# A two-layer trunk on one core: later last quarter products and inner tiles in the MLP batches, plain tiles behind its heads, ada pieces moved

## The chip, the cores and the metric

The kernel runs on one core of a Trainium2 chip. A core has a matrix engine (TensorE, PE in the profile; PEld is its weight load), VectorE (DVE), ScalarE (ACT), GpSimd (POOL) and SyncE (SP), whose queue issues nearly all DMAs here. The metric is the device time of one execution in microseconds (us).

## The reference

Two residual layers on x of 512 positions by 1024 features, in fp32. Cut to what matters:

```python
for layer in range(DEPTH):                      # DEPTH = 2
    mod = c_act @ ada_w[layer] + ada_b[layer]
    shift1, scale1, gate1, shift2, scale2, gate2 = jnp.split(mod[:, None, :], 6, axis=-1)
    h = rms_norm(x, norm_mix[layer]) * (1.0 + scale1) + shift1
    if layer % 2 == 0:
        y = mixer_conv_hgrn(h, ...)             # gated convolution and HGRN2 recurrence
    else:
        y = mixer_stick_breaking(h, ...)        # causal attention without softmax
    x = x + gate1 * y
    h = rms_norm(x, norm_mlp[layer]) * (1.0 + scale2) + shift2
    x = x + gate2 * (jnp.square(jax.nn.relu(h @ mlp_w1[layer])) @ mlp_w2[layer])
```

The MLP of each layer goes from 1024 to 4096 and back. The change lies mostly in it.

## The kernel before

**Products.** Activations lie transposed: 128 features by 512 positions in a tile. Every fp32 product is three matmuls (`mm3`, L276 to L283): both operands are split into a high and a low part, and hi x hi (L281), hi x lo (L282) and lo x hi (L283) are summed in a PSUM bank. A weight tile of 128x1024 (512 KB, eight blocks of 128 columns) is loaded by SP into one of three raw slots (`raw_w`, L258); ACT copies it to the high part (L271), DVE subtracts for the low part (L272); `whi` and `wlo` have four slots each. The split weights start at the slot's first byte (`AT512`) or 64 bytes on (`AT256`, L265): those of products with 512 columns have the first, those with 256 columns the second.

**Ada pieces.** `mod` is made in pieces of 128 outputs: a 512 KB load into a raw slot on SP and one dot on DVE (L420, with a short read of its sum). `background(n)` puts the next n pieces in at its place in the order. In layer 0's mixer there are 4 pieces behind v_g, one behind each of the four lin heads, one behind each lin of the four conv tiles and one at the end of each, and 8 between the first three tiles of the output projection and the fourth. In layer 0's MLP there are two behind each w2 tile until none is left, that is in batches 0 to 2.

**The MLP.** The 32 hidden tiles are made in four batches of eight; after each batch its share of the second product is added to x. Hidden tiles 0 to 3 of a layer are the head (`mlp_head`, L1149, and L1627 for layer 1): by halves of 256 positions, with direct products, while `sums` (L1007) builds from h four tiles of sums t0 to t3 on DVE and ACT. All other hidden tiles come in pairs (`pair`, L1065): a two-by-two Strassen-Winograd scheme makes two hidden tiles with seven quarter products of 12 matmuls of 256 columns (84) in place of 96. Its weights are made on DVE (`pair_w`, sums L1058 to L1062, splits L272). The seven go into three banks a, b and c in this order: hh, t0, t1, hh, hh, t2 and at last t3. ACT copies intermediate sums out, DVE adds them at L1104 and L1106 (both halves of the first tile) and L1109 (the second half of the second tile, from bank a). The seventh product, t3 with `wd`, adds to bank a again, so it waits for L1109. It is deferred: `pair` returns it, and the next pair runs it as `before()` behind its second product. After each half or tile ACT takes relu and square and copies the high part (`hidh`), DVE subtracts (`hidl`, L291).

**A batch's end.** In `mlp` (L1117) the deferred product of the last pair is run by `rest()`, and then the w2 tiles follow: eight in batches 0 to 2, five in batch 3 (the other three are made by halves in the code behind it). Each has eight inner tiles k = 0 to 7 (the batch's hidden tiles), three matmuls of 512 columns each, and then `x_add` (L506, DVE reads the bank), and `background(2)`.

**Order.** In layer 0 and in both MLPs the order on PE is that of the code. On DVE, ACT and SP a scheduler places the instructions, so that a change on PE shifts them. Banks are given by `acc`, which counts up through eight names.

Of the kernel before, what the change touches and what calls it, by code (L numbers as in the profile page):

```python
# [23 lines left out]
P = 128  # L24
T = 512
NT = 8
# [194 lines left out]
def trunk(tc, x_d, c_d, rep_d, small_d, const_d, ada_d, ws_d, win_d, wv_d, woab_d, w1_d, w2_d, wqk_d, wvc_d, woc_d, out_d):  # L221
# [53 lines left out]
    def load_w(src, of=None, at=AT512):  # L275
        return split_w(raw_w(src), of, at)  # L276

    def mm3(ps, w, wc, h, hs, start, stop, **kw):

        whi, wlo = w[0][:, wc], w[1][:, wc]  # L280
        pe.matmul(ps, whi, h[0][:, hs], start=start, stop=False, **kw)  # L281
        pe.matmul(ps, whi, h[1][:, hs], start=False, stop=False, **kw)  # L282
        pe.matmul(ps, wlo, h[0][:, hs], start=False, stop=stop, **kw)  # L283
# [68 lines left out]
    def acc():  # L352
        return mps.tile([P, T], F32, name="acc", tag="acc", bufs=4)
# [94 lines left out]
    def background(n):  # L448
        for _ in range(min(n, len(todo))):
            l, v, f = todo.pop(0)  # L450
            ada_piece(l, v, f)
            if f == 7:
                ada_done(l, v, 0, 8)
# [469 lines left out]
    background(4)  # L923
    for h in range(4):
        run(lin(h, do_hg, h))
        background(1)


    def conv(i):
        p3 = []  # L930
        for r in range(3):
            yield from lin(4 + 3 * i + r, p3.append)
            background(1)
            if r == 0:
                cv = mp.tile([P, T], F32, name="cv", tag="cv", bufs=2)
                act.copy(cv, p3[0])
            elif r == 1:
                u = mp.tile([P, T + 2], F32, name="u", tag="u")
                pool_e.memset(u[:, 0:2], 0.0)
                dve.tensor_tensor(u[:, 2:T + 2], p3[1], cv, op=ALU.mult)  # L940
                cw = [small[:, S_CONV + 4 * r + i:S_CONV + 4 * r + i + 1] for r in range(3)]
                dve.tensor_scalar(cv, u[:, 2:T + 2], cw[2], None, op0=ALU.mult)
                dve.scalar_tensor_tensor(cv, u[:, 1:T + 1], cw[1], cv, op0=ALU.mult, op1=ALU.add)
                dve.scalar_tensor_tensor(cv, u[:, 0:T], cw[0], cv, op0=ALU.mult, op1=ALU.add)
        dve.tensor_tensor(cv, p3[2], cv, op=ALU.mult)
        yy = mp.tile([P, 2, T], F32R, name="yy", tag=f"y{i}")
        yh, yl = yy[:, 0], yy[:, 1]
        split(cv, yh, yl)
        y[i] = (yh, yl)
        background(1)  # L950

    for i in range(4):
        run(conv(i))
# [18 lines left out]
    HALVED = (4, 5, 6, 7)  # L972
    PLACES = {5: (mp, "F2", "Q2"), 6: (mp, "Ft", "Kt")}
    run(proj((0, 1, 2), [load_w(woab_d[o]) for o in (0, 1, 2)], FULL))
    background(8)
    for o in range(3, HALVED[0]):
        run(proj((o,), [load_w(woab_d[o])], FULL))
    ws = {o: load_w(woab_d[o], PLACES.get(o), AT256) for o in HALVED}
# [11 lines left out]


    pp = pool("pp", PSUM)
    bank = [0]

    def acc(n=T):
        bank[0] += 1
# [71 lines left out]
    def pair(l, i, hp, th, hid, before):  # L1068
# [45 lines left out]
            relu2(1, H[0], a)  # L1114
        return last

    def mlp(l, last, hp, head, th):  # L1117

        nrm = Norm(1, 0, (7,)) if not last else None
        for b in range(4):  # L1120
            hid, rest = list(head) if b == 0 else [], lambda: None
            for i in range(len(hid) // 2, 4):
                rest = pair(l, 4 * b + i, hp, th, hid, rest)
            rest()
            for o in range(8 if b < 3 else 5):
                w, ps = load_w(w2_d[l, b // 2, o, b % 2]), acc()
                for k in range(8):
                    mm3(ps, w, ks(k), hid[k], FULL, k == 0, k == 7)
                x_add(o, ps, FULL, l, GATE2)
                if b == 3:  # L1130
                    if last:
                        sync.dma_start(out_d[o], x[o])
                    else:
                        nrm.add(o, FULL)
                background(2)
        if not last:
            log_exp_tables()
        ps, banks, ws = {}, {}, []
        for o in range(5, 8):
            for hf in range(2):  # L1140
                banks[bank[0] % 8] = o, hf
                ps[o, hf] = acc(256)

            ws.append(load_w(w2_d[l, 1, o, 1], None if o == 5 else (hp, f"t{o - 6}h", f"t{o - 6}l"), AT256))
        return nrm, ps, banks, hid, ws
# [480 lines left out]

    w = [weights(w1_d[1, j], None, AT256) for j in range(4)]  # L1627
    for hf, sl in enumerate(H):
        ps = [r.new() for r in (accs, accs, zts, zts)]
        for k, j in by_half(hf, 4):  # L1630
            order.append(mm3h(ps[j], half, w[j], ks(k), (hh[hf][k],), sl, k == 0, k == NT - 1, 256))
        for j in range(4):
            c_, (hi, lo) = cms.new(), hid[j]
            on_act(256, lambda c_=c_, p_=ps[j], sl=sl: act.activation(c_.t[:, sl], half(p_.t), AF.Relu), (ps[j],), (c_,), 0, psum=True)
            on_act(256, lambda c_=c_, sl=sl: act.activation(c_.t[:, sl], c_.t[:, sl], AF.Square), (c_,), (c_,), 0)
            on_act(256, lambda c_=c_, hi=hi, sl=sl: act.copy(hi.t[:, sl], c_.t[:, sl]), (c_,), (hi,), 0)
            on_dve(256, lambda c_=c_, hi=hi, lo=lo, sl=sl: dve.tensor_tensor(lo.t[:, sl], c_.t[:, sl], hi.t[:, sl].bitcast(F32),
                   op=ALU.subtract), (c_, hi), (lo,), 0)
# [87 lines left out]
```

## Time and profile before

| what | value |
|---|---|
| time, median of 3 runs | 1272.83 us (1272.48 to 1274.75) |
| the profiled execution's own time | 1269.31 us |
| its span | 1267.5 us |
| mean granted clock of TensorE | 0.984 |
| PE busy | 1224.1 us (97%) |
| DVE busy, ACT busy | 904.9 us (71%), 622.9 us (49%) |
| DMA | 163.50 MB, mean 129 GB/s |

In the span layer 0's lin and conv tiles lie from about 65 to 216 us, its projection to 263, the head of its MLP to 291.7; its batches end near 319, 406, 493 and 579. The attention of layer 1 starts at about 616, the head of its MLP at 913.8, and its batches end near 966, 1050, 1134 and 1218. A row of a timeline has the start, the duration, the engine, the line, the operation with its output and inputs, the shape, and in brackets the idle time of the engine before it with what ended that. Ends of matmuls are modelled, and they overlap; the step from one start to the next is what a matmul costs.

### The profile page before, as it was taken

Reading aid. Unit: us, or ns where it says so; the run is one execution under the profiler, and the core shown is the slowest. Engines: PE = TensorE matmul, PEld = TensorE weight load, DVE = VectorE, ACT = ScalarE, POOL = GpSimd, SP = SyncE. Lnnn points to the kernel's source line nnn. Section 1 sums busy time; section 2 is a strip of 40 time slices with the busy share of each in tenths; the row PEclk is TensorE's granted clock in tenths of the full one; section 3 lists DMA queues with packets and bytes.
Section 4 is the critical chain, followed back from the end, with each engine's and each line's share of the span. In section 5 each row is a group of like instructions: output and inputs, shape, how many; then the busy total and the mean of one; then the engine's idle time right before and its main releaser. Section 6 shows DMA issues by size and latency. Waiting matters only on the chain.

```text
span 1267.5 us, 19414 instructions
## 1 busy us (share of the span) xinstructions
PE 1224.1 (97%) x7721; PEld 1069.3 (84%) x7721; DVE 904.9 (71%) x1455; ACT 622.9 (49%) x1127; POOL 13.8 (1%) x24
## 2 busy tenths in 40 slices
PE   8999999998999999999999999999889999999998
PEld 6888878988798898898978778777888898998988
DVE  8996859679788688785567773669795575675651
ACT  4433232456247165275458754667465273372650
POOL 0000000000000000000200000000000000000000
PEclk9999999998999999999989999999999999999999
DMA  8664444613745736734132213322013233143141
GB/s 310 245 217 160 139 150 147 202 34 113 252 151 187 252 126 222 239 105 166 51 100 68 67 51 91 93 67 95 31 43 123 77 100 119 65 150 100 52 149 50
DMA packets 46618, 163.50 MB, mean 129 GB/s; under 512 B 5296, under 2 KB 6328, under 8 KB 46528
## 3 DMA queue, kind: packets, MB, share of 16 engines
q1 hardware_dynamic: 46384, 161.78, 38.5%
q8 instruction: 60, 0.98, 0.3%
q10 hardware_dynamic: 144, 0.49, 0.1%
q14 instruction: 30, 0.25, 0.1%
HBM read 155.96 MB, written 2.10 MB: 125 GB/s over the span
## 4 chain that ended last, share of the span: by engine, by line
PE 78%; DVE 12%; DMA 5%; ACT 3%; issue 2%; SPq 0%; DVEq 0%; ACTq 0%
PE b L281 17%; PE b L283 17%; PE b L282 17%; DMA wraw<-in_w 3%; PE acc L281 3%; PE acc L283 3%; PE acc L282 3%; DVE wlo L272 3%; PE acc L652 2%; PE b L1486 1%; PE b L1465 1%; PE b L1521 1%; ACT whi L271 1%; PE b L1385 1%; PE b L1522 1%
## 5 line engine op out<-in xcount | busy, mean ns | idle before, releaser
L271 ACT CAST whi<-wraw 128x1024 fp32r<-128x1024 f32 x123 | 127.8, 1048 | 238.7 <-DMA wraw<-in_w 103.8
L281 PE MATMUL b<-hidh,whi 128*128 128x512 f32 (+1 forms) x560 | 209.1, 373 | 0.0
L282 PE MATMUL b<-hidl,whi 128*128 128x512 f32 (+1 forms) x560 | 208.2, 372 | 0.0
L283 PE MATMUL b<-hidh,wlo 128*128 128x512 f32 (+1 forms) x560 | 207.8, 371 | 0.0
L281 PE MATMUL b<-hh,whi 128*128 128x256 f32 (+1 forms) x624 | 191.7, 307 | 6.2 <-DVE x L506 5.9
L272 DVE TENSOR_TENSOR wlo<-wraw,whi 128x1024 fp32r<-128x1024 f32 x123 | 150.4, 1223 | 61.4 <-ACT whi L271 59.5
L283 PE MATMUL b<-hh,wlo 128*128 128x256 f32 (+1 forms) x624 | 187.2, 300 | 1.9 <-DVE wlo L272 1.9
L282 PE MATMUL b<-hl,whi 128*128 128x256 f32 (+1 forms) x624 | 186.5, 299 | 0.0
L506 DVE SCALAR_TENSOR_TENSOR x<-b,modc,x 128x512 f32<-128x512 f32 (+1 forms) x102 | 68.8, 675 | 105.9 <-PE b L283 105.7
L281 PEld LDWEIGHTS b<-hh,whi 128*128 128x128 f32 x624 | 119.1, 191 | 18.3 <-issue 7.2
L283 PEld LDWEIGHTS b<-hh,wlo 128*128 128x128 f32 x624 | 118.9, 190 | 6.4 <-DVE wlo L272 2.3
L282 PEld LDWEIGHTS b<-hl,whi 128*128 128x128 f32 x624 | 119.8, 192 | 3.1
L282 PEld LDWEIGHTS b<-hidl,whi 128*128 128x128 f32 x560 | 106.1, 190 | 18.0
L281 PEld LDWEIGHTS b<-hidh,whi 128*128 128x128 f32 x560 | 105.8, 189 | 18.2
L283 PEld LDWEIGHTS b<-hidh,wlo 128*128 128x128 f32 x560 | 105.6, 189 | 18.4
L420 DVE CUSTOM_DVE_ANT_0 ascr<-wraw,cb 128x1024 bf16<-128x1024 f32 x80 | 97.8, 1222 | 22.1 <-DMA wraw<-in_ada 21.6
L272 DVE TENSOR_TENSOR wlo<-tt,whi 128x1024 fp32r<-128x1024 f32 x56 | 68.3, 1221 | 18.6 <-ACT whi L271 17.7
L271 ACT CAST whi<-tt 128x1024 fp32r<-128x1024 f32 x56 | 57.3, 1050 | 48.6 <-PE b L282 34.1
L1299 DVE TENSOR_TENSOR wlo<-raw,whi 128x1024 fp32r<-128x1024 f32 x34 | 41.5, 1222 | 21.8 <-ACT whi L1298 21.5
L281 PE MATMUL acc<-hh,whi 128*128 128x512 f32 x128 | 52.2, 408 | 0.0
L1449 DVE TENSOR_TENSOR_SCAN om<-om,pat 128x772 f32<-128x772 f32 (+2 forms) x24 | 46.5, 1936 | 5.8 <-ACT om L1445 5.8
L282 PE MATMUL acc<-hl,whi 128*128 128x512 f32 x128 | 49.9, 390 | 0.0
(376 smaller groups left out, 2709.6 us busy)
## 6 DMA issues: line engine op xcount, KB each, us to landing
wraw<-in_w SPq DMA_DIRECT2D x124, 512.0 KB, 3.4
wraw<-in_ada SPq DMA_DIRECT2D x80, 512.0 KB, 4.3
eraw<-in_ada SPq DMA_DIRECT2D x16, 512.0 KB, 3.9
wraw<-in_win SPq DMA_DIRECT2D x16, 512.0 KB, 3.3
raw<-in_wqk SPq DMA_DIRECT2D x16, 512.0 KB, 3.6
raw<-in_ws SPq DMA_DIRECT2D x8, 512.0 KB, 6.1
wraw<-in_woab SPq DMA_DIRECT2D x8, 512.0 KB, 3.9
raw<-in_wvc SPq DMA_DIRECT2D x8, 512.0 KB, 3.4
```

The costliest lines, as they stand in the source:

```text
L271: act.copy(hi, raw)
L272: dve.tensor_tensor(lo, raw, hi.bitcast(F32), op=ALU.subtract)
L281: pe.matmul(ps, whi, h[0][:, hs], start=start, stop=False, **kw)
L282: pe.matmul(ps, whi, h[1][:, hs], start=False, stop=False, **kw)
L283: pe.matmul(ps, wlo, h[0][:, hs], start=False, stop=stop, **kw)
L420: dve.tensor_tensor_reduce(out=scr, in0=raw, in1=cb, scale=1.0, scalar=0.0, op0=ALU.mult, op1=ALU.add, accum_out=modr[:, col:col + 1])
L506: dve.scalar_tensor_tensor(x[o][:, sl], ps, mcol(l, v, o), x[o][:, sl], op0=ALU.mult, op1=ALU.add)
L652: order.append(on("PE", 8 * 0.000417 * (sl.stop - sl.start), lambda k=k, wi=wi, hi_=hi_, sl=sl, w=w: [pe.matmul(sacc[j][:, sl], w[wi].t[:, ...
L1299: on_dve(1024, lambda: dve.tensor_tensor(lo.t, raw.t, hi.t.bitcast(F32), op=ALU.subtract), (raw, hi), (lo,), 1)
L1385: on_pe(0.13, lambda s=s, sq=sqs[p, s, s0]: pe.matmul(ms.t[64 + 32 * s:96 + 32 * s, sl], hs, sq.t[:, sl], start=True, stop=True), (sqs[p, ...
L1449: on_dve(2 * nw, lambda: dve.tensor_tensor_scan(s_(), s_(), pats[i][:, ::-1], 0.0, op0=ALU.mult, op1=ALU.max), (om,), (om,), 2)
L1465: pe.transpose(tp.t[:, o_:o_ + P], be.t[:, w0:w0 + P], ident)
```

## The change

Six edits:

1. Each of the four lin heads has two ada pieces behind it instead of one, and each conv tile two at its end instead of one; the eight ahead of the projection's fourth tile go. The number of pieces is the same.
2. The counter of bank names in the MLP of layer 0 starts at 4.
3. Hidden tiles 4 and 5 of each layer, right behind the head, are made directly (`whole_tile`): two times 24 matmuls of 512 columns, in place of a pair of 84 with 256.
4. The last deferred product of a batch comes behind inner tiles 0 to 6 of w2 tile 0; then come inner tiles 0 to 6 of w2 tile 1; then inner tile 7 of both, with their x_adds and ada pieces behind.
5. The weights of the last w2 tile of each batch start 64 bytes on.
6. In layer 1's head the fourth accumulator is taken from another ring of banks (`miscs` instead of `zts`).

```diff
     for h in range(4):
         run(lin(h, do_hg, h))
-        background(1)
+        background(2)
...
         y[i] = (yh, yl)
-        background(1)
+        background(2)
...
     run(proj((0, 1, 2), [load_w(woab_d[o]) for o in (0, 1, 2)], FULL))
-    background(8)
...
-    bank = [0]
+    bank = [4]
...
+    def whole_tile(l, j, hp, hid):
+
+        w, ps, c_ = load_w(w1_d[l, j]), acc(), hp.tile([P, T], F32, name="cm", tag="cm", bufs=3)
+        for k in range(NT):
+            mm3(ps, w, ks(k), hT[k], FULL, k == 0, k == NT - 1)
+        hid.append(hid_new(hp, j))
+        act.activation(c_, ps, AF.Relu)
+        act.activation(c_, c_, AF.Square)
+        split(c_, *hid[j])
+
     def mlp(l, last, hp, head, th):
...
             hid, rest = list(head) if b == 0 else [], lambda: None
+            if b == 0:
+                for j in (4, 5):
+                    whole_tile(l, j, hp, hid)
             for i in range(len(hid) // 2, 4):
                 rest = pair(l, 4 * b + i, hp, th, hid, rest)
-            rest()
-            for o in range(8 if b < 3 else 5):
-                w, ps = load_w(w2_d[l, b // 2, o, b % 2]), acc()
-                for k in range(8):
-                    mm3(ps, w, ks(k), hid[k], FULL, k == 0, k == 7)
+            n = 8 if b < 3 else 5
+            second = lambda o: (acc(), load_w(w2_d[l, b // 2, o, b % 2], None, AT256 if o == n - 1 else AT512))
+
+            def products(p, k0, k1):
+                for k in range(k0, k1):
+                    mm3(p[0], p[1], ks(k), hid[k], FULL, k == 0, k == 7)
+
+            def done(o, ps):
                 x_add(o, ps, FULL, l, GATE2)
...
-                background(2)
+                if b < 3:
+                    background(2)
+
+            p0 = second(0)
+            products(p0, 0, 7)
+            rest()
+            p1 = second(1)
+            products(p1, 0, 7)
+            for o, p in enumerate((p0, p1)):
+                products(p, 7, 8)
+                done(o, p[0])
+            for o in range(2, n):
+                p = second(o)
+                products(p, 0, 8)
+                done(o, p[0])
...
-        ps = [r.new() for r in (accs, accs, zts, zts)]
+        ps = [r.new() for r in (accs, accs, zts, miscs)]
```

PE at the end of batch 0 of layer 0, before (`b_2816` is bank a of the last pair):

```order
L282 MATMUL b_2816<-t2l,whi 128x256
L283 MATMUL b_2816<-t2h,wlo 128x256
L281 MATMUL b_2816<-t3h,wdh 128x256
L282 MATMUL b_2816<-t3l,wdh 128x256
L283 MATMUL b_2816<-t3h,wdl 128x256
```

Now (`b_2770` is that bank, `b_2868` the bank of w2 tile 0):

```order
L282 MATMUL b_2770<-t2l,whi 128x256
L283 MATMUL b_2770<-t2h,wlo 128x256
L281 MATMUL b_2868<-hidh,whi 128x512
L282 MATMUL b_2868<-hidl,whi 128x512
L283 MATMUL b_2868<-hidh,wlo 128x512
```

```order
L281 MATMUL b_2868<-hidh,whi 128x512
L282 MATMUL b_2868<-hidl,whi 128x512
L283 MATMUL b_2868<-hidh,wlo 128x512
L281 MATMUL b_2770<-t3h,wdh 128x256
L282 MATMUL b_2770<-t3l,wdh 128x256
L283 MATMUL b_2770<-t3h,wdl 128x256
```

The t3 product stood right behind that of t2 in the same bank; 21 matmuls of 512 columns now stand between them (the first three and the last three are shown).

DVE at the same place, before, from L1104 of the last pair on (`hidl` of 128x512 is the sixth inner tile, counted from 0; the rows of 128x256 are halves of the seventh):

```order
L1104 TENSOR_TENSOR cm<-b_2817,kept 128x256
L272 TENSOR_TENSOR wlo<-wraw,whi 128x1024
L1106 TENSOR_TENSOR cm<-b_2818,kept 128x256
L420 ISA ascr,modr<-wraw,cb 128x1024
L420 ISA modr 128x1
L1109 TENSOR_TENSOR cm<-b_2816,kept 128x256
L420 ISA ascr,modr<-wraw,cb 128x1024
L420 ISA modr 128x1
L291 TENSOR_TENSOR hidl<-cm,hidh 128x512
L291 TENSOR_TENSOR hidl<-cm,hidh 128x256
L272 TENSOR_TENSOR wlo<-wraw,whi 128x1024
L291 TENSOR_TENSOR hidl<-cm,hidh 128x256
```

Now:

```order
L272 TENSOR_TENSOR wlo<-wraw,whi 128x1024
L1104 TENSOR_TENSOR cm<-b_2771,kept 128x256
L420 ISA ascr,modr<-wraw,cb 128x1024
L420 ISA modr 128x1
L1106 TENSOR_TENSOR cm<-b_2772,kept 128x256
L420 ISA ascr,modr<-wraw,cb 128x1024
L420 ISA modr 128x1
L1109 TENSOR_TENSOR cm<-b_2770,kept 128x256
L420 ISA ascr,modr<-wraw,cb 128x1024
L420 ISA modr 128x1
L291 TENSOR_TENSOR hidl<-cm,hidh 128x512
L291 TENSOR_TENSOR hidl<-cm,hidh 128x256
```

The weights of w2 tile 0 have moved ahead of L1104, and a third dot stands between L1104 and the sixth inner tile's low part.

DVE behind the head of layer 0, before, from the last sum of t3 on (first the pair's weights from memory, then the sums for them, with the head's `hidl` rows between):

```order
L1021 TENSOR_TENSOR t3l<-tt,t3h 128x1024
L272 TENSOR_TENSOR wlo<-wraw,whi 128x1024
L1058 TENSOR_TENSOR tt<-wraw 128x512
L291 TENSOR_TENSOR hidl<-cm,hidh 128x256 x2
L1059 TENSOR_TENSOR tt<-tt,wraw 128x512
L291 TENSOR_TENSOR hidl<-cm,hidh 128x256
L1061 TENSOR_TENSOR tt<-wraw,tt 128x512
L291 TENSOR_TENSOR hidl<-cm,hidh 128x256
L1062 TENSOR_TENSOR tt<-wraw 128x512
L272 TENSOR_TENSOR wlo<-tt,whi 128x1024 x2
```

Now:

```order
L1021 TENSOR_TENSOR t3l<-tt,t3h 128x1024
L272 TENSOR_TENSOR wlo<-wraw,whi 128x1024
L291 TENSOR_TENSOR hidl<-cm,hidh 128x256 x4
L272 TENSOR_TENSOR wlo<-wraw,whi 128x1024 x2
L1058 TENSOR_TENSOR tt<-wraw 128x512
L1062 TENSOR_TENSOR tt<-wraw 128x512
L1059 TENSOR_TENSOR tt<-tt,wraw 128x512
```

Between the head and the next pair's sums there are now three splits of weights from memory: those of hidden tiles 4 and 5 and the first of pair 3.

## The prediction, made before the changed kernel was run

> **What bounds the kernel now.** I read the page first, then the list of waits, then 20 us windows, then the timeline of the matrix engine (PE) and of VectorE (DVE) at the places where PE waits. From the page:
>
> ```profile
> span 1267.5 us, 19414 instructions
> PE 1224.1 (97%) x7721; PEld 1069.3 (84%) x7721; DVE 904.9 (71%) x1455; ACT 622.9 (49%) x1127; POOL 13.8 (1%) x24
> ```
>
> PE is the bound: 43 us of the span are without a matmul. A change that leaves the number of matmuls nearly as it is can gain what PE waits, and what it runs slowly after waits. The list of waits (total, times, longest) names four large items that this change touches or could touch:
>
> ```profile
> PE b L281 <- DVE cm L1109: 11.0, 8, 2.5
> PE b L281 <- ACT whi L271: 6.4, 2, 4.4
> PE b L281 <- DVE x L506: 6.1, 3, 3.0
> PE b L283 <- DVE wlo L272: 3.2, 4, 1.6
> ```
>
> The first is one wait at each of the eight batch ends, the second and fourth lie behind the two heads, the third ahead of them. The timeline of PE at the end of batch 0 of layer 0 (start, duration, operation, idle before) has the first:
>
> ```profile
> 315.03 0.28 PE L281 MATMUL b<-t2h,whi 128*128 128x256 f32 x1
> ...
> 316.27 0.28 PE L283 MATMUL b<-t2h,wlo 128*128 128x256 f32 x1
> 318.94 0.58 PE L281 MATMUL b<-t3h,wdh 128*128 128x256 f32 x1 [2.39 <-DVE cm L1109]
> ...
> 321.67 0.63 PE L281 MATMUL b<-hidh,whi 128*128 128x512 f32 x1
> 322.10 0.49 PE L282 MATMUL b<-hidl,whi 128*128 128x512 f32 x1
> 322.43 0.39 PE L283 MATMUL b<-hidh,wlo 128*128 128x512 f32 x1
> 322.66 0.40 PE L281 MATMUL b<-hidh,whi 128*128 128x512 f32 x1
> ...
> 324.73 0.39 PE L281 MATMUL b<-hidh,whi 128*128 128x512 f32 x1
> ...
> 330.17 0.39 PE L281 MATMUL b<-hidh,whi 128*128 128x512 f32 x1
> ```
>
> From start to start, 256 columns take 0.113 us here (11 steps in 1.24), a quarter product of 12 matmuls 1.36; 512 columns take 0.227 (24 in 5.44). The product from t2 ends at 316.38; the one from t3 writes the same bank, which L1109 must have read, and starts 2.56 later. Its twelve matmuls then take 2.73 instead of 1.36, and the next two 512-column ones 0.43 and 0.33: another 1.7. So the end of this batch costs 4.2 us. The windows show the lower granted clock in the same places (PE, PEld, DVE, ACT, POOL busy, PEclk, DMA share, GB/s):
>
> ```profile
> 65.00:85.00 20.00, 20.00 (x113) 17.37 (x111) 19.90 (x35) 5.59 (x9) 0.00 (x0) 1.00 0.64 214
> 85.00:105.00 20.00, 19.26 (x140) 15.98 (x139) 16.96 (x29) 6.72 (x10) 0.00 (x0) 1.00 0.56 185
> 165.00:185.00 20.00, 20.00 (x94) 14.61 (x92) 11.78 (x17) 6.61 (x10) 0.10 (x1) 1.00 0.49 158
> 280.00:300.00 20.00, 15.85 (x120) 14.88 (x120) 20.00 (x36) 16.17 (x35) 0.00 (x0) 0.87 0.07 22
> 300.00:320.00 20.00, 17.61 (x143) 17.41 (x143) 16.84 (x28) 12.37 (x24) 0.00 (x0) 0.93 0.58 189
> 340.00:360.00 20.00, 20.00 (x90) 16.57 (x89) 14.15 (x20) 3.98 (x4) 0.00 (x0) 1.00 0.78 257
> 945.00:965.00 20.00, 18.10 (x144) 17.86 (x144) 15.83 (x23) 14.07 (x24) 0.00 (x0) 0.91 0.43 134
> ```
>
> **The heads: two plain tiles for one pair.** Behind the head of layer 0 DVE is full (20.00 of 20 from 280 to 300), and PE waits for what it makes; behind that of layer 1 PE waits for ACT:
>
> ```profile
> 291.73 0.39 PE L281 MATMUL b<-hh,whi 128*128 128x256 f32 x1
> ...
> 293.84 0.38 PE L283 MATMUL b<-hh,wlo 128*128 128x256 f32 x1 [1.61 <-DVE wlo L272]
> ...
> 297.38 0.58 PE L281 MATMUL b<-t0h,whi 128*128 128x256 f32 x1 [1.99 <-ACT whi L271]
> ...
> 298.73 0.58 PE L283 MATMUL b<-t0h,wlo 128*128 128x256 f32 x1 [0.56 <-DVE wlo L272]
> ```
>
> ```profile
> 940.17 0.28 PE L281 MATMUL b<-hh,whi 128*128 128x256 f32 x1
> ...
> 946.14 0.39 PE L281 MATMUL b<-t0h,whi 128*128 128x256 f32 x1 [4.45 <-ACT whi L271]
> ...
> 964.89 0.28 PE L283 MATMUL b<-t2h,wlo 128*128 128x256 f32 x1
> 966.11 0.38 PE L281 MATMUL b<-t3h,wdh 128*128 128x256 f32 x1 [0.94 <-DVE cm L1109]
> ```
>
> Layer 0, before: from 291.73 to 316.38 are 24.65 us for 13 quarter products, which unhindered are 17.7: 7 us are lost. Now: tile 4 still waits for its first wlo until 293.84, since DVE's row ahead of it (t3l) stays; its other 22 matmuls at 0.227 end at 298.8, tile 5 ends at 304.3, and six quarter products of pair 3 end at 312.4. DVE has two weight splits and the hidl rows instead of the sums of a pair between 293.8 and 297.7, so tile 5 has its weights a microsecond early. That is 4.0 earlier, although two plain tiles cost 10.88 of PE where the pair cost 9.52. In DVE's new order a row of the norm (L491) stands ahead of the last x_add before head(0), for which PE waits there: 0.4 back. **Term: -3.6.** The other bank names change no releaser: the rows that wait for that x_add still do, so the 3.0 us of L506 stay in both heads.
>
> Layer 1, before: 940.17 to 965.0. Now, with both tiles' weights read from memory long before, 940.2 + 10.88 + 8.16 = 959.2, or 0.4 later if 256 columns run at the slower step that is shown below. **Term: -5.6.**
>
> **The batch ends.** The t3 product now comes behind 21 matmuls of w2 tile 0 (4.76 us), so its wait for L1109 is covered. What is late next is the sixth inner tile: k = 6 of w2 tile 0 is due 18 matmuls, 4.08 us, after the t2 product. DVE at the end of batch 0 before:
>
> ```profile
> 316.99 0.42 DVE L1106 TENSOR_TENSOR cm<-b,kept 128x256 f32<-128x256 f32 x1
> 317.32 1.22 DVE L420 CUSTOM_DVE_ANT_0 ascr<-wraw,cb 128x1024 bf16<-128x1024 f32 x1
> ...
> 318.47 0.42 DVE L1109 TENSOR_TENSOR cm<-b,kept 128x256 f32<-128x256 f32 x1
> 318.80 1.22 DVE L420 CUSTOM_DVE_ANT_0 ascr<-wraw,cb 128x1024 bf16<-128x1024 f32 x1
> ...
> 319.94 1.10 DVE L291 TENSOR_TENSOR hidl<-cm,hidh 128x512 fp32r<-128x512 f32 x2
> ```
>
> The low part of tile 6 (the first of the two hidl) was done at about 320.5, 4.1 after the t2 product: just late. In the new order of batch 0 one ada dot more (1.3 us with its read) stands between L1104 and it, and in batches 1 and 2 one more ahead of the weights of w2 tile 1. I leave 1.8 us of the 4.2 in batch 0, and 1.0 in batches 1 and 2: waits of 1 to 2 us, as the 1.61 above, behind which the ten matmuls left of that product had ended by 295.39 (297.38 less 1.99), so at no more than 0.155 each and not the 0.213 of a slow stretch (318.94 to 321.67). Batch 1 now:
>
> ```profile
> 406.26 0.38 PE L281 MATMUL b<-t3h,wdh 128*128 128x256 f32 x1 [2.30 <-DVE cm L1109]
> ```
>
> Batches 0 to 2 have idle times of 2.3 to 2.5 in that list; I give each the 4.2. The other five share 11.0 - 7.2 = 3.8, or 0.8 each, 1.0 from start to start (966.11 above has 1.1): the end of batch 3 and the four of layer 1, with no ada dots ahead. All of that goes. **Term: -(2.4 + 3.2 + 3.2 + 5 x 1.0) = -13.8.** Both x_adds of tiles 0 and 1 come together behind k = 7; they read banks that no one needs for eight tiles, so this is free; with a shorter ring it would cost a tile.
>
> A rule that speaks to this: the Trainium skill's page "TensorE: Matmul & The Clock Gate" (Part 1, and its table on why this matters) has the clock fall to half after an idle window of some 3.4 us and asks for no idle gaps over 3 us. The trace disagrees in size: 2.39 and 1.99 us of idle time were enough for matmuls at about half speed. By the page the ends would be worth their waits alone.
>
> **Ada pieces moved.** Eight pieces (a 512 KB DMA on SP's queue and a dot of 1.22 us on DVE each) go from before the projection into the four lin heads and the four conv tiles, 65 to 216 us; pieces in all are the same.
>
> ```profile
> L420 DVE CUSTOM_DVE_ANT_0 ascr<-wraw,cb 128x1024 bf16<-128x1024 f32 x80 | 97.8, 1222 | 22.1 <-DMA wraw<-in_ada 21.6
> ```
>
> They share three raw slots with the weights, so a weight's load is queued on SP behind them, and a weight's wlo on DVE behind their dots. At the floor this is free: the window 340 to 360 has two pieces to a weight, at 257 GB/s, with PE at 20.00 of 20, and lin and conv have DMA at 0.49 to 0.64. At the ceiling, the lin heads have DVE at 19.90 of 20, and each of their four pieces puts off one wlo by one dot: 4 us in all with the rest. I take **+1.0**, near the floor, as PE has 20.00 in that fullest window. Nothing is won at the projection, where PE does not wait now.
>
> **The last weights of a batch 64 bytes on.** The 256-column products that follow a 512-column stretch without a wait run at a slower step:
>
> ```profile
> 365.53 0.28 PE L281 MATMUL b<-hh,whi 128*128 128x256 f32 x1
> ...
> 368.36 0.28 PE L281 MATMUL b<-t1h,whi 128*128 128x256 f32 x1
> ```
>
> That is 24 matmuls in 2.83, 0.118 each against 0.113. These weights lie 64 bytes on already; what precedes them does not, and would now. Six batches (1 to 3 of each layer) begin so, each with four pairs of 84 matmuls: at most 2016 run at this step, and if it depends on the place, 2016 x 0.0047 = 9.4 us go. If 512-column products lose as much there, eight tiles of 24 cost 0.9. No row shows a 512-column stretch at that place; the one thing near it that the rows show at the quicker step (315.03 above) follows waits. I take **0**.
>
> **Sum.** -3.6 - 5.6 - 13.8 + 1.0 + 0 = -22.0, on the profiled execution of 1269.31 us (span 1267.5): 1247.3. It lies 3.5 under the median of 1272.83; on that, 1250.8.
>
> **The rivals.**
>
> *The step falls too.* The 64 bytes put 256-column products at 0.113 throughout: 1250.8 - 9.4 = 1241.4. For: the same weights run at both steps, so something from before is carried over. Against: no such pair is shown. 0.28.
>
> *The inner tile's wait takes the place of L1109's.* Four ada dots surround L1109 in batch 0, and each may wait for its DMA (L420: 21.6 us over 24 waits). From a wait of about 2.2 us on, the clock falls as now, and batches 0 to 2 keep all of their 4.2: 8.8 of the gain gone, 1259.6. Against: the rows of batch 0 show these dots back to back. 0.14.
>
> *The slow matmuls have another cause and stay.* By the page's rule waits of 2 to 2.5 us would not cause them. Then the waits go, and 1.7 at each of three ends and about 1.7 at each head stay: 8.5 less, 1259.3. Against: the windows' granted clock of 0.87, 0.93 and 0.91, and no slow stretch without such a wait. 0.04.
>
> *Slower: the moved pieces starve lin and conv.* Each of the eight holds SP's queue and a raw slot, and PE waits there as at the heads, over 2.2 us with the slow stretch behind it. It turns the sign from 23.0 / 8 = 2.9 us per piece; at 4.2 each (the price of a batch end), 33.6 - 23.0 = +10.6, 1283.4. For: DVE 19.90 of 20 in lin. Against: DMA at 0.64 at most, and four slots of split weights. 0.06, a third of it so near the turn that it can't be told from no change.
>
> **How the numbers follow.** The forecast has 0.48, with 1246 to 1255 as its own bounds (the pieces 0 to +4, the ends and heads 4 either way). The range takes in the step's case with 2 us of room below, and the two cases at 1259.5 with 2.5 above: 1239.5 to 1262. A change under 0.2% (2.5 us) is about what can't be told from none in this kernel. Faster: all but the last rival, 0.94; same 0.02; slower 0.04.
>
> **What would show it.** In the new profile: no wait for L1109 in the list; waits of PE for hidl (L291) under 2 us at the ends of batches 0 to 2 and none in layer 1; PE's t3 product at 0.113 or 0.118 and PEclk at 1.00 around 320, 400 and 490; one wait of 1.6 behind the head of layer 0, none of 4.4 behind that of layer 1; PE still 20.00 in lin's windows. Steps of 0.113 at the first products of batches 1 to 3 would make the first rival right. A list of waits with wraw or whi in lin and conv, over 2 us each, would make the whole forecast wrong.

## The result, and the profile after

| what | before | changed |
|---|---|---|
| time, median | 1273.19 us (4 runs) | 1266.51 us (4 runs, 1264.80 to 1267.08) |
| profiled execution's span | 1267.5 us | 1265.3 us |
| ratio of the times | | 0.9944, 95% interval 0.9926 to 0.9961 |

(The 1272.83 us further up is the median of three of these four runs.) The change makes the kernel faster by 0.56%, about 7 us. Forecast were 22, with a range that ended at 1262. The page and the list of PE's waits of the changed kernel (total, times, longest) look at first as forecast:

```profile
span 1265.3 us, 19233 instructions
PE 1227.5 (97%) x7649; PEld 1066.8 (84%) x7649; DVE 891.7 (70%) x1435; ACT 616.7 (49%) x1111; POOL 13.8 (1%) x24
```

```profile
PE b L281 <- DVE x L506: 6.5, 3, 3.2
PE b L281 <- ACT whi L271: 4.7, 3, 2.2
PE b L283 <- DVE wlo L272: 4.6, 6, 1.7
...
PE lv L808 <- DVE Kt L839: 2.4, 1, 2.4
...
PE b L282 <- DVE hidl L291: 1.5, 3, 1.1
```

The eight waits for L1109 (11.0 us) are gone, and in their place stand three short ones for hidl (1.5). But there are still three waits for whi and six for wlo, and there is a new one for Kt. To find where they lie, the two traces are set side by side by stage, with the starts of PE's first matmul in each (us). "Pairs" is the first pair of a batch; further down, "w2" is the first inner tile of a batch, which before comes behind the t3 product and now ahead of it.

| start of | before | changed | later by |
|---|---|---|---|
| projection | 217.75 | 225.10 | 7.35 |
| head, layer 0 | 263.00 | 270.35 | 7.35 |
| pairs of batch 1 | 365.53 | 368.16 | 2.63 |
| pairs of batch 2 | 452.93 | 453.60 | 0.67 |
| pairs of batch 3 | 539.69 | 544.36 | 4.67 |
| last three w2 tiles, layer 0 | 607.45 | 615.57 | 8.12 |
| pairs of batch 1, layer 1 | 1011.12 | 1011.20 | 0.08 |
| last matmul | 1263.91 | 1261.64 | -2.27 |

Three things are seen: 7.4 us are lost ahead of the projection (about 1.5 of it in the first 60 us, which the change does not touch); layer 0's MLP wins 6.7 until the pairs of batch 2 and loses 7.4 by its end; from there on layer 1 wins 10.4. Cut at the ends of the t2 products, layer 0's MLP shows where: its four w2 parts (from the end of the last t2 product of a batch to the next pairs, or to the last three w2 tiles) are 10.4 quicker together, and the pairs of batches 1 to 3 (up to that t2 product) are 13.2 slower.

**What happens at a batch's end, and behind it.** PE in batch 0 of layer 0 (timeline; start, duration, operation, idle before): the t2 product ends and w2 tile 0 follows at once, waits a microsecond for the sixth inner tile, and the t3 product runs at full speed behind (12 matmuls in 1.36):

```profile
321.59 0.28 PE L283 MATMUL b<-t2h,wlo 128*128 128x256 f32 x1
...
327.27 0.50 PE L282 MATMUL b<-hidl,whi 128*128 128x512 f32 x1 [1.07 <-DVE hidl L291]
327.61 0.40 PE L283 MATMUL b<-hidh,wlo 128*128 128x512 f32 x1
327.85 0.28 PE L281 MATMUL b<-t3h,wdh 128*128 128x256 f32 x1
```

That is what the prediction said. One batch later, PE at the first pair of batch 2, and then of batch 3:

```profile
453.60 0.28 PE L281 MATMUL b<-hh,whi 128*128 128x256 f32 x1
454.45 0.38 PE L283 MATMUL b<-hh,wlo 128*128 128x256 f32 x1 [0.45 <-DVE wlo L272]
458.07 0.38 PE L281 MATMUL b<-t0h,whi 128*128 128x256 f32 x1 [2.20 <-ACT whi L271]
459.33 0.58 PE L283 MATMUL b<-t0h,wlo 128*128 128x256 f32 x1 [0.76 <-DVE wlo L272]
```

```profile
544.95 0.38 PE L283 MATMUL b<-hh,wlo 128*128 128x256 f32 x1 [0.20 <-DVE wlo L272]
548.57 0.39 PE L281 MATMUL b<-t0h,whi 128*128 128x256 f32 x1 [2.20 <-ACT whi L271]
549.83 0.38 PE L283 MATMUL b<-t0h,wlo 128*128 128x256 f32 x1 [0.76 <-DVE wlo L272]
```

Before, there was no wait at these places. A slow stretch follows the first, with 256 columns at 0.21 us each until 465.3; the granted clock is the number ahead of the last two:

```profile
460.00:462.00 2.00, 2.00 (x11) 2.00 (x11) 2.00 (x3) 0.57 (x3) 0.00 (x0) 0.50 0.74 291
```

So from the first pair of batch 2 to its last t2 product PE takes 45.1 us, where it took 37.6. DVE ahead of the first wait, in the changed kernel, shows why the weights are late (the ada dots are L420, the splits of weights L272, a pair's sums begin with L1058):

```profile
446.48 1.23 DVE L272 TENSOR_TENSOR wlo<-wraw,whi 128x1024 fp32r<-128x1024 f32 x1 [1.98 <-ACT whi L271]
...
449.52 1.21 DVE L420 CUSTOM_DVE_ANT_0 ascr<-wraw,cb 128x1024 bf16<-128x1024 f32 x1
...
453.17 1.23 DVE L272 TENSOR_TENSOR wlo<-wraw,whi 128x1024 fp32r<-128x1024 f32 x1 [2.03 <-ACT whi L271]
454.32 0.74 DVE L506 SCALAR_TENSOR_TENSOR x<-b,modc,x 128x512 f32<-128x512 f32 x1
454.98 0.68 DVE L1058 TENSOR_TENSOR tt<-wraw 128x512 f32<-128x512 f32 x1
```

The pair's first weights are split at 453.17; in the profile of before that row stands at 447.06. The x_add between the split and the pair's sums puts those off by another 0.66. ACT, for which DVE waits, waits itself for the load:

```profile
445.40 1.05 ACT L271 CAST whi<-wraw 128x1024 fp32r<-128x1024 f32 x1 [5.67 <-DMA wraw<-in_w]
452.09 1.05 ACT L271 CAST whi<-wraw 128x1024 fp32r<-128x1024 f32 x1 [5.64 <-DMA wraw<-in_w]
```

From one weight to the next, with two ada pieces between them, are 6.7 us here, and PE uses up one in 5.44. The loads fall behind PE in the course of the w2 part. The windows of the three w2 parts show a nearly full PE and an even rate of loading (PE, PEld, DVE, ACT, POOL busy, PEclk, DMA share, GB/s):

```profile
324.00:360.00 36.00, 34.93 (x160) 28.85 (x159) 26.11 (x41) 8.65 (x12) 0.00 (x0) 1.00 0.76 246
409.00:452.00 43.00, 42.77 (x194) 35.16 (x194) 30.32 (x49) 9.64 (x14) 0.00 (x0) 1.00 0.77 249
500.00:543.00 43.00, 42.76 (x194) 35.19 (x194) 29.78 (x47) 9.58 (x14) 1.39 (x1) 1.00 0.78 253
```

A batch's w2 part has 8 weights and 16 pieces, 24 loads of 524,288 bytes; at 249 GB/s that is 50.5 us. Its matmuls take 44.9 (8 x 5.44 and the t3 product's 1.41), and the part from 407.89 to 453.60 took 45.7. Before, the wait for L1109 with its slow stretch lay in the same part, and from the end of the t2 product (403.8) to the pairs of batch 2 (452.93) were 49.1 us. By this the old wait at the batch's end was time in which the loads caught up; the experiments test it.

**Lin and conv.** DVE in a conv tile of the changed kernel, and PE behind it:

```profile
141.82 1.23 DVE L420 CUSTOM_DVE_ANT_0 ascr<-wraw,cb 128x1024 bf16<-128x1024 f32 x1 [2.82 <-DMA wraw<-in_ada]
142.97 0.09 DVE L420 DVE_READ_ACCUMULATOR2_ANT modr<- 128x1 f32 x1
142.97 1.28 DVE L825 COPY_PREDICATED A<-lvl,lv 128x256 f32<-128x256 uint8 x2
144.06 0.71 DVE L839 TENSOR_TENSOR Kt<-Kt,T 128x512 f32<-128x512 f32 x1
```

```profile
144.92 3.65 PE L808 MATMUL lv<-Q,Kt 128*128 128x64 f32 x16 [2.38 <-DVE Kt L839]
```

```profile
145.00:165.00 20.00, 19.55 (x122) 16.78 (x123) 17.06 (x27) 2.29 (x4) 0.10 (x1) 0.84 0.38 129
```

An ada dot waits 2.8 us for its load, Kt stands behind it on DVE, and PE waits 2.4 us for Kt; in the next window the granted clock is 0.84 where it was 1.00 before. The slow stretch behind such a wait isn't in every execution. The same wait, 2.38 at 145.05, stands in the trace of the kernel with the 64 bytes undone (an experiment below), and there the clock stays at 1.00; first the window of the changed kernel, then that one's:

```profile
146.00:148.00 2.00, 2.00 (x12) 2.00 (x11) 2.00 (x4) 0.00 (x0) 0.00 (x0) 0.50 0.27 66
146.00:148.00 2.00, 2.00 (x15) 1.83 (x14) 2.00 (x4) 0.00 (x0) 0.00 (x0) 1.00 0.21 63
```

**The heads.** Behind the head of layer 1 there is no wait left: tile 4 starts at 946.67, pair 3 at 957.58 and the t2 product ends at 966.06, 19.4 us in all, where it was 24.8. Behind that of layer 0 one wait is left, as forecast, but a slow stretch follows it:

```profile
298.69 0.50 PE L281 MATMUL b<-hh,whi 128*128 128x512 f32 x1
...
301.09 0.50 PE L283 MATMUL b<-hh,wlo 128*128 128x512 f32 x1 [1.67 <-DVE wlo L272]
...
305.07 0.39 PE L281 MATMUL b<-hh,whi 128*128 128x512 f32 x1
```

```profile
300.00:302.00 2.00, 0.91 (x3) 0.76 (x4) 1.71 (x3) 1.22 (x5) 0.00 (x0) 0.89 0.00 0
302.00:304.00 2.00, 2.00 (x6) 1.52 (x6) 0.76 (x2) 2.00 (x6) 0.00 (x0) 0.50 0.80 262
304.00:306.00 2.00, 2.00 (x9) 1.61 (x8) 1.97 (x2) 1.47 (x2) 0.00 (x0) 0.75 0.00 0
```

Here too the length of the wait doesn't settle it. In the kernel with the moved pieces undone (below) the same row waits as long, and the matmuls behind it take 0.23 us each:

```profile
294.18 0.50 PE L283 MATMUL b<-hh,wlo 128*128 128x512 f32 x1 [1.67 <-DVE wlo L272]
```

```profile
296.00:298.00 2.00, 2.00 (x11) 1.65 (x10) 1.50 (x3) 2.00 (x4) 0.00 (x0) 1.00 0.43 168
```

**The 64 bytes.** The last w2 tile of a batch, and the pair behind it, in layer 1:

```profile
1005.60 0.40 PE L281 MATMUL b<-hidh,whi 128*128 128x512 f32 x1
...
1010.74 0.40 PE L282 MATMUL b<-hidl,whi 128*128 128x512 f32 x1
1010.97 0.39 PE L283 MATMUL b<-hidh,wlo 128*128 128x512 f32 x1
1011.20 0.28 PE L281 MATMUL b<-hh,whi 128*128 128x256 f32 x1
```

Its 24 matmuls take 5.60 us in place of 5.44, and the pairs behind still run at 0.118.

### The profile page after: what moved, and what is told of

The parts are those of the page before. It is cut to its first block, busy times and chain, and to the rows that moved or that the text cites. A ratio compares the mean times of both kernels' runs of the same rounds, so it can differ in the third digit from the quotient of the medians.

```text
span 1265.3 us, 19233 instructions
## 1 busy us (share of the span) xinstructions
PE 1227.5 (97%) x7649; PEld 1066.8 (84%) x7649; DVE 891.7 (70%) x1435; ACT 616.7 (49%) x1111; POOL 13.8 (1%) x24
## 4 chain that ended last, share of the span: by engine, by line
PE 73%; DVE 10%; DMA 10%; ACT 4%; issue 2%; SPq 0%; ACTq 0%; DVEq 0%
PE b L281 16%; PE b L283 16%; PE b L282 16%; DMA wraw<-in_w 6%; DVE wlo L272 4%; DMA wraw<-in_ada 3%; PE acc L281 3%; PE acc L283 3%; PE acc L282 3%; ACT whi L271 2%; PE acc L652 2%; PE b L1495 1%; PE b L1516 1%; PE b L1551 1%; PE b L1415 1%
## 5 line engine op out<-in xcount | busy, mean ns | idle before, releaser
L281 PE MATMUL b<-hh,whi 128*128 128x256 f32 (+1 forms) x632 | 197.7, 313 | 7.0 <-DVE x L506 6.3
L272 DVE TENSOR_TENSOR wlo<-wraw,whi 128x1024 fp32r<-128x1024 f32 x125 | 152.1, 1222 | 62.9 <-ACT whi L271 61.4
L283 PE MATMUL b<-hh,wlo 128*128 128x256 f32 (+1 forms) x632 | 193.2, 306 | 2.3 <-DVE wlo L272 2.3
L282 PE MATMUL b<-hl,whi 128*128 128x256 f32 (+1 forms) x632 | 192.8, 305 | 0.0
L506 DVE SCALAR_TENSOR_TENSOR x<-b,modc,x 128x512 f32<-128x512 f32 (+1 forms) x102 | 68.1, 675 | 88.6 <-PE b L283 88.5
L420 DVE CUSTOM_DVE_ANT_0 ascr<-wraw,cb 128x1024 bf16<-128x1024 f32 x80 | 97.8, 1222 | 31.0 <-DMA wraw<-in_ada 30.8
L272 DVE TENSOR_TENSOR wlo<-tt,whi 128x1024 fp32r<-128x1024 f32 x52 | 63.5, 1222 | 19.7 <-ACT whi L271 19.0
L271 ACT CAST whi<-tt 128x1024 fp32r<-128x1024 f32 x52 | 53.2, 1049 | 41.5 <-PE b L282 25.3
L291 DVE TENSOR_TENSOR hidl<-cm,hidh 128x256 fp32r<-128x256 f32 (+1 forms) x90 | 44.5, 510 | 20.1 <-ACT hidh L290 19.3
```

The costliest lines, as they stand in the source:

```text
L271: act.copy(hi, raw)
L272: dve.tensor_tensor(lo, raw, hi.bitcast(F32), op=ALU.subtract)
L291: dve.tensor_tensor(lo[:, sl], t_[:, sl], hi[:, sl].bitcast(F32), op=ALU.subtract)
L420: dve.tensor_tensor_reduce(out=scr, in0=raw, in1=cb, scale=1.0, scalar=0.0, op0=ALU.mult, op1=ALU.add, accum_out=modr[:, col:col + 1])
L506: dve.scalar_tensor_tensor(x[o][:, sl], ps, mcol(l, v, o), x[o][:, sl], op0=ALU.mult, op1=ALU.add)
```

## The experiments

The theory after the traces: the terms of the prediction for heads and ends are right by themselves, but (1) the eight moved pieces cost some 6 us in lin and conv, and (2) the loads of layer 0's w2 parts are the next bound, so that what the ends save there is paid at the next batch's first pair. Rivals: the waits at the pairs come from the new order of DVE's rows; the ends were never worth what was forecast; the wait for Kt is chance. All ratios are against the kernel before on the same chip.

**The moved pieces undone.** From the changed kernel:

```diff
         run(lin(h, do_hg, h))
-        background(2)
+        background(1)
...
-        background(2)
+        background(1)
...
+    background(8)
     for o in range(3, HALVED[0]):
```

> The changed kernel with the eight ada pieces back ahead of the projection's fourth tile. In the changed kernel PE waits 2.5 us for Kt (L839) at 144.9 us and runs slowly behind it, and its projection is 7.4 us later than before, 1.5 of it from the start. Theory: the moved pieces made that wait; without them about 5.9 us go, 1260.6 us. Rival: the wait comes by chance or with the new order as such; 1266 us, and the wait at L839 stays.

Measured: 1260.58 us, ratio 0.9892 (0.9865 to 0.9920), where the changed kernel has 0.9944. The wait for Kt is gone and the projection starts at 217.96, 0.2 later than before. That is 0.52% or 6.6 us for the eight pieces. The theory holds: the wait is not chance, since it is 2.38 and 2.50 long near 145 in the traces of two other kernels with all eight pieces moved (64 bytes undone, and pieces spread, below). Its slow stretch is in neither of these, and their projections start 4.9 and 5.3 later than here; in the changed kernel's trace it is 7.1.

**Half of them undone.** The four pieces of the conv tiles back (the lin heads' kept), or those of the lin heads back (the conv tiles' kept), each time with `background(4)` ahead of the projection's fourth tile:

> The changed kernel with the four pieces of the conv tiles back ahead of the projection's fourth tile, those of the lin heads kept. If the lin heads' pieces make the wait for Kt near 145 us (DVE is fullest there), it stays and the time is 1265 us; if the conv tiles' pieces make it, it goes: 1261 us.

> The changed kernel with the four pieces of the lin heads back ahead of the projection's fourth tile, those of the conv tiles kept. If the lin heads' pieces make the wait for Kt near 145 us, it goes and the time is 1261 us; if the conv tiles' pieces make it, it stays: 1265 us.

Measured: with the lin heads' pieces kept 1259.12 us, 0.9886 (0.9851 to 0.9922), projection at 218.00; with those of the conv tiles kept 1263.04 us, 0.9909 (0.9877 to 0.9941), projection at 220.96. The wait of 2.4 us near 145 is in neither; with the conv tiles' pieces alone PE has three waits for Kt of 0.7 at most, 1.7 together. So neither half makes the wait by itself, which is not what either expectation said; it is seen only where all eight are moved, and not in all such traces (the longest wait for Kt is 0.9 in the control with shorter slots below). The lin heads' four alone cost nothing that shows. The intervals of the two overlap; that the conv tiles' half costs more rests on the two traces.

**Only the batch ends.** The kernel before with only the fourth edit (the last weights at the first byte):

```diff
-            rest()
-            for o in range(8 if b < 3 else 5):
...
+            p0 = second(0)
+            products(p0, 0, 7)
+            rest()
+            p1 = second(1)
+            products(p1, 0, 7)
```

> The kernel before with only the batch ends changed (t3 product behind inner tiles 0 to 6). Theory of the loads: in batches 0 to 2 of layer 0 eight weights and sixteen ada pieces take 49 us at 2.04 us each, as long as the w2 part with its old wait, so what the ends save in layer 0 is paid at the first pair of the next batch (waits of 2.4 us for whi with a slow stretch); layer 1 and batch 3 keep about 4.5: 1266 to 1272 us. Rival, the prediction's: all of 13.8 us go, 1259 us.

Measured: 1274.19 us, ratio 1.0003 (0.9988 to 1.0018): no gain at all, and less than the 1266 to 1272 that the theory expected. PE's waits in its profile:

```profile
PE b L281 <- ACT whi L271: 13.7, 7, 4.4
PE b L283 <- DVE wlo L272: 7.0, 9, 1.9
```

Before, these were 6.4 in two and 3.2 in four waits; the waits for L1109 (11.0) are gone, and 11.1 have come for weights. Layer 1 still gains: between the t2 product of its batch 0 and its last w2 tiles PE is 3.9 us quicker. Layer 0 gives that back and more: its last w2 tiles begin 6.4 later than before. The prediction's 13.8 is refuted for this kernel.

**The pieces spread.** From the changed kernel, the same 48 pieces over four batches:

```diff
-                if b < 3:
-                    background(2)
+                background(2 if b == 3 or o < (5, 5, 4)[b] else 1)
```

> The changed kernel with the 48 ada pieces of layer 0's MLP spread over all four batches: 13, 13, 12 and 10 in place of 16, 16, 16 and 0, so that a w2 part has 21 loads or fewer, 43 us at 2.04 each, under its 45. Theory of the loads: the waits for whi at the first pairs of batches 1 to 3 and their slow stretches go, about 12 us less than the changed kernel, 1254 us. Rival: these waits come from the order of DVE's rows (x_adds ahead of the sums) and stay; 1266 us.

Measured: 1255.88 us, ratio 0.9859 (0.9834 to 0.9885), 0.85% or 10.8 us better than the changed kernel. No wait for whi is left in MLP 0. A w2 part, with loads at less than the rate above:

```profile
404.00:446.00 42.00, 42.00 (x192) 34.81 (x191) 31.31 (x48) 12.80 (x18) 0.00 (x0) 1.00 0.73 237
488.00:530.00 42.00, 42.00 (x192) 34.91 (x191) 30.59 (x45) 12.40 (x17) 0.00 (x0) 1.00 0.73 236
```

```profile
PE b L281 <- DVE x L506: 6.4, 3, 3.2
...
PE lv L808 <- DVE Kt L839: 3.9, 4, 2.5
...
PE b L283 <- DVE wlo L272: 1.4, 1, 1.4
```

The waits for Kt are still there, since the eight pieces are. DVE's rows come in another order too, since the scheduler sets it, and an x_add still stands between the first sums; but the pair's first split is at 440.30, 7.8 us ahead of the pairs of batch 2 (448.11), where it was 0.4 ahead of them in the changed kernel (453.17 and 453.60). There it was a load that ACT waited for, and of DVE's rows only the x_add's 0.66. The rival falls.

**Ends and spreading, and spreading alone, on the kernel before.**

> The kernel before with the batch ends changed and the 48 ada pieces of the MLP spread 13, 13, 12, 10. Theory of the loads: with the loads thinned out the ends keep what they save, the 13.8 us of the prediction's term: 1258 us, and no waits for whi at the first pairs of batches 1 to 3. Rival: the ends are worth only the 4.5 us of layer 1 and batch 3: 1267.5 us.

> The kernel before with only the 48 ada pieces spread 13, 13, 12, 10. Theory of the loads: its batch ends still wait for L1109, and in that time the loads catch up, so fewer loads win little: 0 to 5 us, from dots that no longer stand ahead of L1109; 1267 to 1272 us. Rival: the spreading is what gained in the run with the changed kernel, by itself, 10 us or more: 1262 us or less.

Measured: both 1259.81 us, 0.9883 (0.9858 to 0.9909); spreading alone 1270.18 us, 0.9973 (0.9953 to 0.9992). Spreading alone wins 3 us and keeps its waits:

```profile
PE b L281 <- DVE cm L1109: 11.1, 8, 2.4
```

With both, no wait for whi is left at the first pairs of batches 1 to 3. The ends on top of the spreading win another 0.90% or 11.5 us; on the kernel before as it was they won nothing. Neither is worth much without the other: as long as one of the two waits, for L1109 or for loads, is left, it hides most of what the other's removal saves.

**Only the tiles.** The kernel before with `whole_tile` and its call:

```diff
+            if b == 0:
+                for j in (4, 5):
+                    whole_tile(l, j, hp, hid)
```

> The kernel before with only hidden tiles 4 and 5 made directly. Theory: layer 1 gains 5.4 and layer 0 1.6 as in the changed kernel's trace, 1266 us, with the waits for L1109 as before. Rival, the prediction's: 9.2 us, 1264 us.

Measured: 1261.68 us, ratio 0.9912 (0.9887 to 0.9937), 11.2 us. In its trace layer 1 gains 6.2 between the last w2 tiles of layer 0 and w2 of its first batch, and layer 0 gains 3.8 from the start of the head to w2 of its first batch. The gain is above both expectations. Layer 0's is the prediction's 3.6 rather than this theory's 1.6: the wait that is left there is 1.37 in this trace, with no slow stretch behind it.

**Bank names and 64 bytes undone,** one at a time, from the changed kernel.

> The changed kernel with the two bank edits undone. Theory: they change names and no wait; 1266.5 us within 2, and waits of PE for x_add (L506) as in the changed kernel. Rival: the new names are what keep the wait of layer 0's head at 3.3 us and would make it longer or shorter by over 1 us.

> The changed kernel with the last weights of each batch back at the first byte. In the changed kernel's trace 256-column products still begin at 0.118 us, and the 24 matmuls of such a w2 tile take 0.230 to 0.232 instead of 0.227. Theory: the edit only costs, 8 x 24 x 0.004 = 0.8 us; without it 1265.7 us, and no other step changes. Rival: it does quicken some products, and time rises by 2 us or more.

Measured: banks 1265.62 us, 0.9936 (0.9920 to 0.9953), as the changed kernel; the waits for L506 are 6.5 us in three, also as there. 64 bytes: 1262.70 us, 0.9917 (0.9895 to 0.9939), whose interval overlaps that of the changed kernel (0.9926 to 0.9961). That the edit costs 0.16 us a batch, 1.3 in all, is read from the trace; the times can't tell that from nothing.

**A fourth raw slot.** To make room the slots of the split weights were cut from 1088 to 1040 columns; a control has the shorter slots with three raw slots.

> The changed kernel with four raw slots for weights and ada pieces instead of three, the order of all engines unchanged (the slots of the split weights are 192 bytes shorter to make room). Theory of the slots: a load starts when one of three slots comes free, and a slot's round of 6.1 us (4.4 to 4.6 to land, then ACT's copy and DVE's row) limits the loads to one in 2.04 us; with a fourth slot the waits for whi at the first pairs of batches 1 to 3 go, about 12 us less, 1254 us. Rival: the DMA engines' 250 to 260 GB/s are the limit; loads land later and the time stays at 1266.

> The changed kernel with the split weights' slots 192 bytes shorter and still three raw slots: the order of all engines as in the changed kernel. Theory: the shorter slots put the weights at other places, and steps of 0.229 and 0.119 us in place of 0.227 and 0.113 to 0.118, as in the run with four raw slots, cost some 5 us in all; 1271 us. Then the fourth raw slot alone was worth the difference to its 1267. Rival: the places don't matter and it runs as the changed kernel, 1266 us; then four raw slots were worth nothing.

Measured: four slots 1267.42 us, 0.9961 (0.9947 to 0.9975); control 1265.87 us, 0.9946 (0.9925 to 0.9966). The first expectation was wrong in that the scheduler, which knows the slots, did change the order on DVE and ACT (not on PE and SP). The control kept the order of the changed kernel, and moved 251 and 261 GB/s in the two windows below. A second run of the four slots, meant to stand beside the control on one chip, gave no time, so the two are compared through their ratios. By these the fourth slot is worth nothing in time. In its trace the waits for whi at the three first pairs are gone (PE's waits for whi are 4.7 in three in the changed kernel and 2.0 in two in the control, so the shorter slots alone took part of them away), and the loads run quicker at about the same DMA share:

```profile
409.00:452.00 43.00, 41.84 (x187) 34.04 (x186) 36.70 (x59) 13.17 (x18) 0.00 (x0) 1.00 0.77 272
494.00:538.00 44.00, 42.16 (x189) 34.27 (x188) 37.79 (x59) 13.77 (x19) 2.26 (x1) 1.00 0.79 273
```

At 272 GB/s 24 loads are 46.3 us, still over 44.9; new waits for hidl (2.6 in two) stand in the w2 parts of batches 1 and 2, and one of 3.3 for whi behind the head. So slots are likely a part of the limit; since the order of DVE and ACT changed with the fourth, that is not shown apart from the order, and whether the slots or the DMA engines set the rest stays open. What is shown, by the spread pieces, is that fewer loads in the w2 parts take these waits away.

**All that helped, together.** The changed kernel with the pieces back, the spreading, and the last weights at the first byte:

> The changed kernel with the eight moved ada pieces put back, the 48 pieces of the MLP spread over four batches, and the last weights back at the first byte. If the three terms add up: 1255.9 (spread) - 5.6 (pieces back) - 0.8 = 1249.5 us. Rival: what the pieces cost in conv was already hidden by the loads' limit further on, and it stays near 1256.

Measured: 1250.36 us, ratio 0.9827 (0.9811 to 0.9843). It beats both kernels: 22 us under the kernel before, 15 under the changed one. In its profile PE has no wait for whi, Kt's are 0.8 us together, and those for hidl 0.9.

## Why the prediction was wrong

The direction was right and the size was not: 7 us instead of 22.

- **The heads** (-3.6 and -5.6): right. The tiles alone gained 11.2 us, with 3.8 and 6.2 in the trace; in the changed kernel's profile layer 1 has its 5.4 (24.8 to 19.4) and layer 0 about 2, since a slow stretch follows the wait of 1.67.
- **The batch ends** (-13.8): the mechanism was right at each end. The four w2 parts of layer 0 became 10.4 us quicker, where its ends had 9.8 of the term (2.4 + 3.2 + 3.2 + 1.0), and on top of the spreading the ends are worth 11.5. The step that failed is the one behind: "What is late next is the sixth inner tile". That was late by 1.1 us, less than the 1.8 allowed for it; but next after it were the weights of the following pair, whose waits and slow stretches made the pairs of batches 1 to 3 13.2 slower. The prediction looked for the next releaser within 4 us of the removed wait and not at the end of the part. Alone, the edit gained nothing.
- **The evidence that was misread** is the window 340 to 360 of before: two pieces to a weight, 257 GB/s, PE 20.00 of 20. It was taken as proof that such a rate of loads is free. It showed that PE was fed, out of split weights that had been made ahead, not that loads kept pace: 24 loads at 257 GB/s are 49.0 us, and the w2 part had 49.1 only with the 4.2 of its wait. The prediction never set the loads' time against the part's.
- **The moved pieces** (+1.0, bounds 0 and +4): measured 6.6, outside the bounds. This is the second term that failed, by its size. It was taken near the floor on that same window. The mechanism of the last rival was right in kind, a piece that keeps DVE from the work behind it, at one place instead of eight: Kt stood on DVE behind a dot whose load was late, PE waited 2.4 for it, and in the profiled execution a slow stretch came on top. With four of the eight pieces the long wait didn't arise.
- **The last weights** (0): right within noise; the bound of 0.9 for a loss was the likelier end, 1.3 by the trace. The first rival, that the step falls to 0.113, is refuted: it stays at 0.118.
- **The bank names** (no releaser changes): right.
- **The rival that an inner tile's wait takes the place of L1109's** named the right shape, a wait in place of a wait, and gave 1259.6; it had the wrong taker. The forecast's own condition for failing, waits for whi over 2 us, was set for lin and conv only; they came, but at the first pairs.
- **Waits of 1 to 2 us run on at full speed**: wrong as a rule. 1.67 us at 301.09 was followed by 3.3 us of matmuls at half speed; 1.07 at 327.27 was not, and the same 1.67 with the moved pieces undone (294.18) was not either. The other way round, 4.2 us for each end of batches 0 to 2 counted on a slow stretch behind each wait of over 2 us, as the profiled execution had it; in the traces above the same wait of 2.38 has one and has none. The Trainium skill's page "TensorE: Matmul & The Clock Gate" (Part 1, and the table under "Why this matters for your kernels") speaks of a free-running window of some 3.4 us and of half the clock, and advises no gaps over about 3 us. The length of that stretch (301.7 to 305.1) and the granted clock of 0.50 agree; the advice does not cover 1.67.

As a sum of timed differences, without the 64 bytes: spreading -3.4, tiles -11.2, ends -11.5 and the moved pieces +6.6 make -19.5, where the changed kernel with the spreading measured -17.9; with the loads as the change has them, 10.8 come back, and -7 are left.

## What to carry to other kernels

Before a wait is removed, look for every stream of loads that catches up during it, and set the loads of the stage times their measured interval against the stage's time without the wait. A stage whose engine is 100% busy out of a store made ahead says nothing about whether the supply keeps pace; look at the first use behind the stage. And background work that waits for a load of its own must not stand on the same engine ahead of something that the bound engine needs: here one late load, 2.8 us on DVE, became 2.4 us of PE, and in some executions a slow stretch.

## What the runs showed of the hardware that was not expected

- The matmul's step is not set by its shape alone. 24 matmuls of 512 columns took 5.44 us with weights at the slot's first byte and 5.60 with them 64 bytes on; with the 64 bytes undone they took 5.44 again. 256-column products took 0.113 or 0.118 us with weights at the same offset; why is open. Where the slots are 4160 instead of 4352 bytes long, 24 matmuls of 512 columns took 5.44 to 5.60 in both kernels that have them, with no effect on the time that could be told.
- With four slots to load into instead of three, the same queue moved 272 and 273 GB/s, where the changed kernel had 249 and 253 and the control 251 and 261, at a DMA share of 0.77 to 0.79 in all: the share of busy DMA engines did not say how much more could be moved.
- The same wait of TensorE can have a stretch at half clock behind it or none. 2.38 us for Kt near 145 was followed by a granted clock of 0.50 in the changed kernel and of 1.00 with the 64 bytes undone; with the pieces spread it was 2.50 and the clock stayed at 1.00 too. 1.67 us behind layer 0's head was followed by 0.50 in the changed kernel and by 1.00 with the moved pieces or the 64 bytes undone. What decides it is not shown here.
